# Three steps moved in the order of a one-core hybrid decoder layer: the first pair's scan products, the squares of the second hidden tile of a pair, and the first output transpose

## The chip, the cores and the metric

One core of a Trainium2 chip runs one inference step of a decoder layer. The metric is the device time of one execution in microseconds (us); lower is better. The kernel before takes 1161.29 us (median of three runs, 1161.14 to 1161.82).

## What is computed

512 prompt tokens and 8 sample tokens, 520 columns in all, go through one layer with a width of 1024. Cut to what matters here:

```python
proj = u @ w_in                      # u: normalized, modulated x
# branch B: xBC -> causal conv4 + SiLU -> x, B, C; chunked scan
states = einsum('bcsgn,bcsgr,bcsgrp->bcgrpn', B, decay_end, x)
y_diag = einsum('bcgrqs,bcsgrp->bcqgrp', wts, x)
y_off  = einsum('bcqgn,bcqgr,cbgrpn->bcqgrp', C, exp(acs), h_in)
x = x + gate1 * (merged @ w_o)
u2 = rmsnorm(x) * (1 + scale2) + shift2
x = x + gate2 * (square(relu(u2 @ w_mlp1)) @ w_mlp2)
out = rmsnorm(x)
```

The scan works on 32 heads in 16 pairs, in four chunks of 128 tokens. The hidden width of the MLP is 4096.

## The kernel before, in words

**Orientation.** Activations lie transposed: 128 features on the partitions, 520 tokens in the free dimension. Every float32 product is made of three products of a split into a high and a low part (`hi`, `lo` of the activations, `wh`, `wl` of the weights). ScalarE (ACT) copies the high part, VectorE (DVE) subtracts it for the low part.

**Windows and quarters.** The work is a list of windows (`win`, line 252), each the product of one 128-column weight block with all tokens. A window has four quarters of 12 matmuls (`one`, line 1306). After each quarter `run` (line 352) calls what was hung on it with `at` (line 349); a slot is 4 times the window's number plus the quarter. The dictionary `PLAN` (line 35) holds slots relative to a window. The engines' programs are in the order in which these calls are made: `manual_schedule` is set for all engines, and an engine that waits holds up all that is behind it on the same engine.

**The start of the scan.** Windows 4 and 5 make the x of pairs 0 and 1. Their evacuation `xbc_evac` (line 368) runs in the first quarter of the next window: two ACT copies out of PSUM and three DVE convolution steps. Then, by `PLAN`, come `finish` (a small DVE step on the samples' columns, then SiLU on ACT), `scan1`, `scan2` and `scan3`. `scan1` (line 435) transposes the pair's four chunks on TensorE into `ptx` and makes two DVE products, `xdec` (by `dd`, the decay to the chunk's end) and `xdt` (by dt). `scan2` (line 446) makes the chunk states `pst` from `xdec`, and `hc` from them (one ACT copy, six DVE steps). `scan3` (line 459) makes `pyd` and `pyo`, the latter from `hc`. `scan_w` (line 417) makes the decays between tokens: DVE subtracts, GpSimd (POOL) masks, ACT takes the exponential; `scan_m` (line 431) multiplies them by the masked products of B and C. For pair 0, `scan1` stands at 12 quarters behind window 4's start, in one slot with `scan_w(0)` and behind it.

**The MLP.** The first product of the MLP is made in four parts of 1024 hidden columns. In the last three of them (`f` = 1 to 3) two windows at a time are made by `seven` (line 1337) with seven half-size products, p = 0 to 6, four such pairs in each part. The products accumulate in three PSUM banks, y, x and w (`yb`, `xb`, `wb`), in the order y, x, w, y, x, w, x. Between them results are copied or added out: after p = 0 ACT copies y to `s1` (trace: `su`), after p = 1 and 2 DVE makes `u2_` and `s15`, after p = 3 ACT writes half of the first hidden tile `r0`, after p = 4, 5 and 6 DVE adds the rest of the hidden tiles `r1` and `r0`. As p = 3 goes on in bank y, it can't start before `s1` is copied. `squares` (line 1344) is three ACT instructions: ReLU, square, and the copy `hi`; `m1_lo` (line 790) is the DVE subtraction `lo`. A pair's weights are four blocks t = 0 to 3, split two products ahead by `split_s` (line 292); for t = 0 and t = 2, DVE first makes two sums of weight blocks (`ss`). The list `later` carries what is left over to the next pair or to `two` (line 1320), which makes the first two windows of the second product of the MLP.

The order of DVE around the end of a pair is: last addition to `r1`; `lo` of `r0`; two `wl` (t = 1); then, of the next pair, two `ss` (t = 2); `lo` of the last pair's `r1`; two `wl` (t = 2); `u2_`; `s15`; one `wl` (t = 3). The order of ACT is: squares of `r0`; two `wh` (t = 1); squares of `r1`; then, of the next pair, two `wh` from the sums (t = 2); the copy `su`; one `wh` (t = 3).

**The end.** `m2_evac` (line 803) adds the last part of the MLP to x in place (`x2`) and hangs up `finish_tile` (line 856): five transposes on TensorE and five small DVE products by the last norm's weight (`yo`). For output block 0 it stands in the last quarter of the second of the two windows of `two`, for blocks 1 and on in the second quarter of the window behind the block's own.

Of the kernel before, what the change touches and what calls it, by code (L numbers as in the profile page):

```python
# [34 lines left out]
PLAN = {'silu': [5, 10],  # L35
 'decay': [12, 15],
 'decay_load': 5,
 'mask': [14, 15],
 'tok': [12, 15],
 'state': [15, 21],  # L40
 'out': [19, 25],
 'bc_silu': [7, 7],
 'bc': [12, 12],
# [29 lines left out]
def tile_hybrid_step(  # L73
# [32 lines left out]
    def act(name, dtype=F32):  # L106
        return ap.tile([P, SLOT], dtype, name=nm(name), tag="act", bufs=NSLOT)
# [7 lines left out]
    def aux(name):  # L115
        return pp.tile([P, 512], F32, name=nm(name), tag="aux", bufs=4)
# [4 lines left out]
    def halves(ap_):  # L121
        return ap_.rearrange("p (h c) -> p h c", h=2)

    def chunks(ap_):
        return ap_.rearrange("p (c q) -> p c q", c=NC)

    def tt(out, in0, in1, op):
        V.tensor_tensor(out=out, in0=in0, in1=in1, op=op)  # L128

    def stt(out, in0, scalar, in1, op0=ALU.mult, op1=ALU.add):  # L130
        V.scalar_tensor_tensor(out=out, in0=in0, scalar=scalar, in1=in1, op0=op0, op1=op1)  # L131
# [7 lines left out]
    def a_copy(out, in_, func=AF.Copy, **kw):  # L139
        S.activation(out=out, in_=in_, func=func, **kw)  # L140

    def mm(out, lhsT, rhs, start=True, stop=True, **kw):
        PE.matmul(out, lhsT=lhsT, rhs=rhs, start=start, stop=stop, **kw)  # L143
# [105 lines left out]
    hooks, mid, end = {}, 1, 3  # L249
# [99 lines left out]
    def at(q, w, fn, *args):  # L349
        hooks.setdefault(4 * w + q, []).append((fn, args))  # L350
# [13 lines left out]
    xbc, szt = {}, {}  # L364
# [3 lines left out]
    def xbc_evac(ps, w, t):  # L368
        raw, cv = act("raw"), act("cv")
        views = ([(halves(raw[:, 0:T]), halves(cv[:, 0:T]), ps[:, :, 0:TH])] if not isinstance(ps, list) else  # L370
                 [(raw[:, h * TH:(h + 1) * TH], cv[:, h * TH:(h + 1) * TH], ps[h][:, 0:TH]) for h in range(2)])
        for r_, c_, p_ in views:
            a_copy(r_, p_)
            a_copy(c_, p_, AF.Identity, scale=par2[:, 72 + t:73 + t], bias=par("cbb", t))
        for k in (2, 1, 0):
            stt(cv[:, 3 - k:NP], raw[:, 0:NP - 3 + k], par2[:, 24 * k + t:24 * k + t + 1], cv[:, 3 - k:NP])
        V.tensor_copy(out=rst[:, :, t], in_=raw[:, NP - 3:T])
        xbc[t] = cv

        def finish():  # L380
            stt(cv[:, NP:T], raw[:, NP:T], par2[:, 72 + t:73 + t], pb[:, t, :])
            a_copy(cv[:, 0:T], cv[:, 0:T], AF.Silu)
            if t < 16:
                V.tensor_copy(out=xs_all[:, :, t], in_=cv[:, NP:T])
            else:
                g, dst = t % 4, bexp if t < 20 else cexp
                V.tensor_copy(out=dst[:, :, 4 * g:4 * g + 4], in_=cv[:, NP:T].unsqueeze(2).to_broadcast([P, NS, 4]))
        if t < 16:
            e = t % 2
            for key, f, args in (("silu", finish, ()), ("tok", scan1, (t,)), ("state", scan2, (t,)), ("out", scan3, (t,))):  # L390
                at(PLAN[key][e], w - e, f, *args)
        else:
            at(PLAN["bc_silu"][w > 4], w, finish)
            if t >= 20:
                at(PLAN["bc"][w > 4], w, bc_group, t - 20)
# [13 lines left out]
    scan, acb = {}, {}  # L409
# [5 lines left out]
            SY.dma_start(out=acb[j][h], in_=ascr[2 * j + h].partition_broadcast(P))  # L415

    def scan_w(j):
        st = scan[j] = {}
        pab = acb.pop(j)
        e2 = st["e2"] = act("e2")  # L420
        segs = st["seg"] = [act("seg") for _ in range(2)]
        for h in range(2):
            hd, rows, sv = 2 * j + h, slice(64 * h, 64 * h + 64), chunks(segs[h][:, 0:NP])
            tt(sv, chunks(pab[h]), acs[:, :, hd:hd + 1].to_broadcast([P, NC, P]), ALU.subtract)
            G.affine_select(out=sv, in_=sv, pattern=[[0, NC], [1, P]], compare_op=ALU.is_ge, fill=-1e30,  # L425
                            base=0, channel_multiplier=-1)
            a_copy(e2[rows, 0:384], pab[h][rows, P:NP], AF.Exp)
        for h in range(2):
            a_copy(segs[h][:, 0:NP], segs[h][:, 0:NP], AF.Exp)
# [3 lines left out]
            tt(seg[:, 0:NP], seg[:, 0:NP], cbm[j // 4][:, 0:NP], ALU.mult)  # L433

    def scan1(j):
        hv, xT_, st = slice(2 * j, 2 * j + 2), xbc[j], scan[j]
        ptx = aux("ptx")
        for c in range(NC):
            PE.transpose(ptx[:, c * P:(c + 1) * P], xT_[:, c * P:(c + 1) * P], ident)
        pv = ptx.rearrange("p (c h e) -> p c h e", c=NC, h=2)  # L440
        for key, f in (("xdec", dd), ("xdt", dtt)):
            st[key] = act(key)
            tt(st[key][:, 0:NP].rearrange("p (c h e) -> p c h e", c=NC, h=2), pv,
               f[:, 0:NC, hv].unsqueeze(3).to_broadcast([P, NC, 2, 64]), ALU.mult)
# [184 lines left out]
    def add_square(acc, t, first, n=T):  # L629
        d = acc if first else act("sqt")  # L630
        a_copy(d[:, 0:n], t[:, 0:n], AF.Square)
        if not first:
            tt(acc[:, 0:n], acc[:, 0:n], d[:, 0:n], ALU.add)
# [67 lines left out]
    def residual(x_, xo, ps, prm, o):  # L701
        t = small([P, NS], "rs")
        tt(t, ps[:, 1, NP - TH:TH], msm(prm, o), ALU.mult)
        tt(t, t, xo[:, NP:T], ALU.add)
        stt(halves(x_[:, 0:T]), ps[:, :, 0:TH], mp(prm, o), halves(xo[:, 0:T]))
        V.tensor_copy(out=x_[:, NP:T], in_=t)
# [83 lines left out]
    def m1_lo(r, hi, lo):  # L790
        tt(lo[:, 0:T], r[:, 0:T], hi.bitcast(F32)[:, 0:T], ALU.subtract)
        hm.append((hi, lo))
# [10 lines left out]
    def m2_evac(ps, w, o, half):  # L803
        residual(x2[o], x2[o], ps, 5, o)
        if half:
            if o == 0:
                sqf.insert(0, act("sqf"))
            add_square(sqf[0], x2[o], o == 0)
            if o == KT - 3:
                V.memset(vf, 1.0)  # L810
                at(end, w + 1, row_means, sqf, 1.0 / D, vf)
            at(mid if o else end, w + 1, finish_tile, o)

    sqf = []
    vf = const([P, 5], "vf")
# [100 lines left out]
    for f in range(4):  # L916
# [5 lines left out]
        for k in range(KT):  # L922
            win("m2", D * f, 256 * (k // 2), k % 2, lambda f=f: hm[8 * f:8 * f + 8],
                lambda ps, w, k=k, f=f: m2_evac(ps, w, k, f == 3))
# [156 lines left out]
    def par(key, i, n=1):  # L1081
        return par1[:, P1[key] + i:P1[key] + i + n]
# [217 lines left out]
    later = []  # L1300

    def evac(n):
        if wins[n][3]:
            wins[n][3](ps_of.pop(n), n)
# [32 lines left out]
    def seven(n):  # L1337
        y, x, w = (aux(z)[:, 0:TH] for z in ("yb", "xb", "wb"))
        banks = (y, x, w, y, x, w, x)
        su, s15, r0, r1 = act("su"), act("s15"), act("relu"), act("relu")  # L1340
        s1, u2_ = su[:, 0:TH], su[:, TH:T]
        hl = [(act("hi", F32R), act("lo", F32R)) for _ in range(2)]

        def squares(r, hi, c0):
            a_copy(r[:, c0:T], r[:, c0:T], AF.Relu)
            a_copy(r[:, 0:T], r[:, 0:T], AF.Square)
            a_copy(hi[:, 0:T], r[:, 0:T])

        def after(p):
            if p == 0:  # L1350
                a_copy(s1, y)
                while later:
                    later.pop(0)()
                evac(n - 1)
            elif p == 1:
                tt(u2_, x, s1, ALU.add)
            elif p == 2:
                tt(s15[:, 0:TH], w, s1, ALU.add)
            elif p == 3:
                a_copy(r0[:, 0:TH], y, AF.Relu)  # L1360
            elif p == 4:
                tt(r1[:, TH:T], x, s15[:, 0:TH], ALU.add)
            elif p == 5:
                tt(r0[:, TH:T], w, u2_, ALU.add)
                squares(r0, hl[0][0], TH)
            else:
                tt(r1[:, 0:TH], x, s1, ALU.add)
                m1_lo(r0, *hl[0])
                squares(r1, hl[1][0], 0)
                later.append(lambda: m1_lo(r1, *hl[1]))  # L1370

        for p in range(7):
            splits_to(unit_of[n] + p // 2 + 2, p % 2 == 1)
            (hi, lo), c = splits[n, p // 2], 4 * (p % 2)
            for k in range(4):
                xh, xl = terms[p][k]
                for i, (w_, x_) in enumerate(((hi, xh), (hi, xl), (lo, xh))):
                    mm(banks[p], w_[:, c + k, :], x_, p < 3 and k == 0 and i == 0, k == 3 and i == 2,
                       skip_group_check=True)
            after(p)  # L1380
            run(n + p // 4, p % 4)
        splits_to(unit_of[n] + 5)
        run(n + 1, 3)
# [61 lines left out]
```

## Time and profile before

| | |
|---|---|
| median of the runs | 1161.29 us |
| the profiled execution: time | 1163.04 us |
| the profiled execution: span from first to last instruction | 1161.3 us |
| TensorE busy (matmuls) | 1128.1 us, 97%, 9554 |
| VectorE busy | 809.0 us, 70%, 1566 |
| ScalarE busy | 497.5 us, 43%, 780 |
| GpSimd busy | 46.1 us, 4%, 85 |
| granted TensorE clock | 0.997 |

PE is TensorE, PEld its weight loads, DVE VectorE, ACT ScalarE, POOL GpSimd, SP SyncE. In a timeline a row gives the start (us), the duration (us), the engine, the line of the helper, the operation, what it writes and reads, and how many alike follow each other; in brackets how long the engine sat idle before it, and what ended that. As helpers record most operations, most rows have the same few lines, and the names of the tiles tell them apart. The profiled execution took 1.74 us more than its span.

### The profile page before, as it was taken

How to read it: one execution, taken by the hardware profiler on the slowest of the kernel's cores; microseconds unless marked ns; L12 is line 12 of the kernel's file. 1: busy time of each engine (PE TensorE's matmuls, PEld its weight loads, DVE VectorE, ACT ScalarE, POOL GpSimd, SP SyncE). 2: the span in 40 equal slices, each digit the busy share in tenths (PEclk: the TensorE clock that was granted, in tenths of full speed). 3: DMA queues.
4: the chain of work that ended last, by engine and by line, in shares of the span. 5: the costliest groups of instructions: out<-in, count | busy, mean ns of one | idle time of the engine just before them, and what ended most of it. 6: DMA issues, size and time to landing. Idle time of an engine off the chain costs nothing.

```text
span 1161.3 us, 22937 instructions
## 1 busy us (share of the span) xinstructions
PE 1128.1 (97%) x9554; PEld 1092.7 (94%) x9554; DVE 809.0 (70%) x1566; ACT 497.5 (43%) x780; POOL 46.1 (4%) x85
## 2 busy tenths in 40 slices
PE   6999999999999999999999999999999999999997
PEld 5798999999998888999999999999999999999996
DVE  5677888678888587888567334578777647657764
ACT  5456555455552222234443222345536515524622
POOL 3001111011110000000000000003000000000000
PEclk9999999999999999999999999999999999999999
DMA  9924333333348996567563243332222332332302
GB/s 280 326 74 132 114 115 96 94 112 114 114 147 292 324 329 199 178 187 212 171 230 101 95 165 124 114 124 97 81 96 73 109 110 73 109 110 73 104 7 74
DMA packets 137747, 164.96 MB, mean 142 GB/s; under 512 B 7144, under 2 KB 107961, under 8 KB 137636
## 3 DMA queue, kind: packets, MB, share of 16 engines
q1 hardware_dynamic: 137116, 162.85, 42.9%
q8 instruction: 75, 1.23, 0.4%
q0 software_dynamic: 528, 0.66, 0.2%
q14 instruction: 28, 0.23, 0.1%
HBM read 145.26 MB, written 18.45 MB: 141 GB/s over the span
## 4 chain that ended last, share of the span: by engine, by line
PE 83%; ACT 6%; DVE 6%; DMA 3%; issue 1%; SPq 1%; ACTq 0%; DVEq 0%
PE ps L143 72%; DMA wa<-in_w_ada_dram 2%; ACT wh L140 2%; DVE wl L128 2%; ACT relu L140 2%; PE xb L143 1%; PE pada L143 1%; PE pyd L143 1%; PE pst L143 1%; PE pyo L143 1%; PE yb L143 1%; ACT hi L140 1%; PE wb L143 1%; DVE cv L131 1%; DVE ss L128 1%
## 5 line engine op out<-in xcount | busy, mean ns | idle before, releaser
L143 PE MATMUL ps<-hi,wh 128*128 128x260 f32 (+2 forms) x2432 | 501.7, 286 | 2.4 <-ACT cv L140 1.1
L143 PE MATMUL ps<-lo,wh 128*128 128x260 f32 (+2 forms) x2432 | 493.3, 283 | 1.7 <-DVE lo L128 1.4
L143 PE MATMUL ps<-hi,wl 128*128 128x260 f32 (+2 forms) x2432 | 491.0, 282 | 0.0
L143 PEld LDWEIGHTS ps<-hi,wh 128*128 128x128 f32 x2432 | 375.2, 188 | 18.1 <-issue 13.6
L143 PEld LDWEIGHTS ps<-lo,wh 128*128 128x128 f32 x2432 | 376.5, 188 | 3.3 <-DVE lo L128 3.3
L143 PEld LDWEIGHTS ps<-hi,wl 128*128 128x128 f32 x2432 | 376.0, 188 | 0.0
L140 ACT ACTIVATE wh<-wt 128x1024 fp32r<-128x1024 f32 (+1 forms) x191 | 183.1, 960 | 318.3 <-PE ps L143 301.9
L128 DVE TENSOR_TENSOR wl<-wt,wh 128x1024 fp32r<-128x1024 f32 (+1 forms) x191 | 210.4, 1103 | 66.2 <-ACT wh L140 66.2
L131 DVE SCALAR_TENSOR_TENSOR cv<-raw,par,cv 128x511 f32<-128x511 f32 (+2 forms) x72 | 54.0, 750 | 10.9 <-ACT cv L140 9.0
L128 DVE TENSOR_TENSOR rs<-ps,mod 128x8 f32<-128x8 f32 x40 | 6.6, 164 | 62.4 <-PE ps L143 62.4
L140 ACT ACTIVATE wh<-ss 128x512 fp32r<-128x512 f32 x48 | 28.7, 621 | 31.7 <-PE ps L143 26.0
L143 PE MATMUL xb<-hi,wl 128*128 128x260 f32 x144 | 40.8, 283 | 0.0
L143 PE MATMUL xb<-hi,wh 128*128 128x260 f32 x144 | 40.7, 283 | 0.0
L143 PE MATMUL xb<-lo,wh 128*128 128x260 f32 x144 | 40.5, 282 | 0.0
L140 ACT ACTIVATE relu<-relu 128x520 f32<-128x520 f32 (+2 forms) x56 | 29.4, 525 | 20.0 <-DVE relu L128 19.2
L425 POOL TENSOR_SCALAR_AFFINE_SELECT seg<-seg 128x512 f32<-128x512 f32 x32 | 24.9, 801 | 299.6 <-DVE seg L128 243.9
L143 PE MATMUL yb<-hi,wh 128*128 128x260 f32 x96 | 28.1, 293 | 8.2 <-ACT su L140 8.2
L140 ACT ACT_TABLE_LOAD x27 | 34.6, 1283 | 2.9 <-DVE cv L131 1.7
L140 ACT ACTIVATE cv<-cv 128x520 f32<-128x520 f32 x24 | 15.3, 639 | 43.1 <-DVE cv L131 43.1
L128 DVE TENSOR_TENSOR wl<-ss,wh 128x512 fp32r<-128x512 f32 x48 | 31.8, 683 | 0.0
L143 PE MATMUL pada<-wa,cT 128*32 128x128 f32 (+1 forms) x384 | 29.0, 400 | 1.1 <-DMA wa<-in_w_ada_dram 0.9
L131 DVE SCALAR_TENSOR_TENSOR x<-ps,mod,x 128x520 f32<-128x520 f32 (+1 forms) x34 | 24.7, 727 | 5.7 <-PE ps L143 4.6
(312 smaller groups left out, 1332.9 us busy)
## 6 DMA issues: line engine op xcount, KB each, us to landing
wt<-in_w_in_dram SPq DMA_DIRECT2D x38, 1024.0 KB
wt<-in_w_mlp_dram SPq DMA_DIRECT2D x32, 1024.0 KB
wa<-in_w_ada_dram SPq DMA_DIRECT2D x96, 256.0 KB
acb<-ascr SPq DMA_DIRECT2D x32, 256.0 KB
hn<-in_state_ssm_dram SPq DMA_DIRECT2D x32, 256.0 KB
out_dram<-hn SPq DMA_DIRECT2D x32, 256.0 KB
wt<-in_w_b_out_dram SPq DMA_DIRECT2D x8, 1024.0 KB
gscr<-sg SPq DMA_DIRECT2D x16, 260.0 KB
```

The lines of the kernel that those rows point to most:

```text
L128: V.tensor_tensor(out=out, in0=in0, in1=in1, op=op)
L131: V.scalar_tensor_tensor(out=out, in0=in0, scalar=scalar, in1=in1, op0=op0, op1=op1)
L140: S.activation(out=out, in_=in_, func=func, **kw)
L143: PE.matmul(out, lhsT=lhsT, rhs=rhs, start=start, stop=stop, **kw)
L425: G.affine_select(out=sv, in_=sv, pattern=[[0, NC], [1, P]], compare_op=ALU.is_ge, fill=-1e30, base=0, channel_multiplier=-1)
```

## The change

Three things are moved. Nothing is added to or taken from the computation.

- `scan1` of pair 0 goes from 12 to 9 quarters behind window 4's start, from the slot behind `scan_w(0)` to one ahead of `finish` of pair 1.
- In `seven`, the squares of `r1` no longer stand at the end of their own pair but in the next one, behind the copy `su` (after p = 0); `lo` of `r1` goes from after p = 0 to after p = 2 of the next pair. Behind the last pair of a part both come after the first quarter of `two`.
- `finish_tile` of output block 0 goes to the slot of block 1's, ahead of it.

```diff
@@ PLAN
+ 'tok0': 9,
@@ xbc_evac
-                at(PLAN[key][e], w - e, f, *args)
+                at(PLAN["tok0"] if key == "tok" and t == 0 else PLAN[key][e], w - e, f, *args)
@@ scan_w
-        st = scan[j] = {}
+        st = scan.setdefault(j, {})
@@ scan1
-        hv, xT_, st = slice(2 * j, 2 * j + 2), xbc[j], scan[j]
+        hv, xT_, st = slice(2 * j, 2 * j + 2), xbc[j], scan.setdefault(j, {})
@@ m2_evac
-            at(mid if o else end, w + 1, finish_tile, o)
+            at(mid, w + (1 if o else 2), finish_tile, o)
@@ seven, after(p)
             if p == 0:
                 a_copy(s1, y)
-                while later:
+                if later:
                     later.pop(0)()
                 evac(n - 1)
             elif p == 1:
                 tt(u2_, x, s1, ALU.add)
             elif p == 2:
                 tt(s15[:, 0:TH], w, s1, ALU.add)
+                while later:
+                    later.pop(0)()
...
                 tt(r1[:, 0:TH], x, s1, ALU.add)
                 m1_lo(r0, *hl[0])
-                squares(r1, hl[1][0], 0)
+                later.append(lambda: squares(r1, hl[1][0], 0))
                 later.append(lambda: m1_lo(r1, *hl[1]))
```

## Rows read from the trace of the kernel before

**Rows 1.** The page, part 1: busy time and share of each engine.

```profile
PE 1128.1 (97%) x9554; PEld 1092.7 (94%) x9554; DVE 809.0 (70%) x1566; ACT 497.5 (43%) x780; POOL 46.1 (4%) x85
```

**Rows 2.** Waits: who waited for whom, us in total, times, longest.

```profile
PE yb L143 <- ACT su L140: 8.2, 9, 0.9
```

**Rows 3.** Timeline of PE, end of window 7 to the start of window 9.

```profile
100.16 1.16 PE L143 MATMUL pst<-xdec,btok 128*128 128x128 f32 x8 [2.22 <-DVE xdec L128]
...
108.47 0.94 PE L143 MATMUL pyo<-cv,hc 128*128 128x128 f32 x6
...
109.27 0.48 PE L143 MATMUL ps<-hi,wh 128*128 128x260 f32 x2
```

**Rows 4.** Timeline of DVE, the same stretch and what leads to it.

```profile
93.79 0.22 DVE L131 SCALAR_TENSOR_TENSOR cv<-raw,par,pb 128x8 f32<-128x8 f32 x1
...
99.43 0.68 DVE L128 TENSOR_TENSOR xdec<-ptx,dd 128x512 f32<-128x512 f32 x1
100.03 0.68 DVE L128 TENSOR_TENSOR xdt<-ptx,dtt 128x512 f32<-128x512 f32 x1
...
107.08 1.23 DVE L131 SCALAR_TENSOR_TENSOR hc<-hc,cd,pst 128x64 f32<-128x64 f32 x6
```

**Rows 5.** Timeline of ACT, the same stretch.

```profile
94.09 1.28 ACT L140 ACT_TABLE_LOAD   x1 [1.67 <-DVE cv L131]
...
106.32 0.26 ACT L140 ACTIVATE hc<-pst 128x128 f32<-128x128 f32 x1
...
107.89 0.60 ACT L140 ACTIVATE sz<-ps 128x520 f32<-128x520 f32 x1
```

**Rows 6.** Windows: length, then busy us (count) of PE, PEld, DVE, ACT, POOL.

```profile
872.60:882.67 10.07, 10.07 (x86) 10.07 (x85) 7.18 (x15) 4.36 (x9) 0.00 (x0) 1.00 0.31 100
...
1079.07:1090.30 11.23, 10.31 (x84) 10.11 (x85) 9.80 (x20) 7.92 (x16) 0.00 (x0) 1.00 0.28 95
```

**Rows 7.** Timeline of PE, p = 3 of the last pair of the third part.

```profile
1090.30 0.39 PE L143 MATMUL yb<-hi,wh 128*128 128x260 f32 x1 [0.92 <-ACT su L140]
```

**Rows 8.** Timeline of ACT, from the end of one pair into the next.

```profile
1084.26 1.09 ACT L140 ACTIVATE relu<-relu 128x260 f32<-128x260 f32 x2 [1.25 <-DVE relu L128]
...
1086.97 1.29 ACT L140 ACTIVATE relu<-relu 128x520 f32<-128x520 f32 x2
1088.30 0.64 ACT L140 ACTIVATE hi<-relu 128x520 fp32r<-128x520 f32 x1
1088.84 1.13 ACT L140 ACTIVATE wh<-ss 128x512 fp32r<-128x512 f32 x2
1089.88 0.36 ACT L140 ACTIVATE su<-yb 128x260 f32<-128x260 f32 x1
1090.15 0.62 ACT L140 ACTIVATE wh<-wt 128x512 fp32r<-128x512 f32 x1
```

**Rows 9.** Timeline of DVE, the same stretch.

```profile
1083.80 0.42 DVE L128 TENSOR_TENSOR relu<-wb,su 128x260 f32<-128x260 f32 x1
...
1086.05 0.70 DVE L128 TENSOR_TENSOR lo<-relu,hi 128x520 fp32r<-128x520 f32 x1 [0.51 <-ACT hi L140]
1086.67 0.68 DVE L128 TENSOR_TENSOR wl<-ss,wh 128x512 fp32r<-128x512 f32 x1
...
1088.48 0.68 DVE L128 TENSOR_TENSOR ss<-wt,ss 128x512 f32<-128x512 f32 x1
1089.08 0.69 DVE L128 TENSOR_TENSOR lo<-relu,hi 128x520 fp32r<-128x520 f32 x1
...
1091.57 0.68 DVE L128 TENSOR_TENSOR wl<-wt,wh 128x512 fp32r<-128x512 f32 x1
```

**Rows 10.** Timeline of PE, transposes of output block 1.

```profile
1112.84 0.66 PE L864 MATMUL pt<-ident,x 128*128 128x128 f32 x4 [1.48 <-DVE x L131]
```

**Rows 11.** Timeline of DVE, output blocks 0 and 1.

```profile
1110.65 0.88 DVE L128 TENSOR_TENSOR yo<-pt,gbc 128x128 f32<-128x128 f32 x4
...
1112.02 0.76 DVE L131 SCALAR_TENSOR_TENSOR x<-ps,mod,x 128x520 f32<-128x520 f32 x1
```

## The prediction

> **What bounds the kernel now.** I read the page's busy times first: TensorE is busy 97% of the span, so time is to be had only where it stands idle [rows 1]. The view of waits names where it waits for another engine: nine times for ScalarE's copy `su`, in all 8.2 us, each about 0.9 [rows 2]. There are twelve pairs in `seven`, four in each of three parts; nine of them have another pair ahead, so it is one wait for each boundary between pairs, at p = 3, as the last of them at 1090.30 shows [rows 7]. The timeline of PE shows two more long waits that the diff touches: 2.22 us for `xdec` ahead of the first `pst` [rows 3], and 1.48 us for the updated x ahead of the transposes of output block 1 [rows 10]. These three places are all that the change can win from, some 13 us with the restarts. What matters is what comes last behind each wait once the named one is gone, so for each I laid the queues of DVE and ACT out in the new order, with the durations and steps of the rows; an engine works its instructions off in the order written.
>
> **The boundary between pairs (the large term).** The change takes three ACT instructions, the squares of `r1`, from ahead of `su` and puts them behind it. The windows view says who is full there: from one stall to the next, 11.23 us, DVE is busy 9.80 and ACT 7.92; a first pair, which has no stall, takes 10.07 [rows 6]. So I follow DVE. Call the start of its second `ss` S (1088.48). Its end, S + 0.68, releases the second of the two `wh` copies that stand ahead of `su` on ACT. Before, this copy starts one step behind the first (1.13 for both, less 0.62 for one: 0.51), at 1089.35, or S + 0.87, because the squares had kept ACT until 1088.84 [rows 8, 9]. Without them it starts when the sum is there, with 0.03 for the hand-over (1083.80 + 0.42 to 1084.26 is one) at S + 0.71, and `su` at S + 1.23 where it was S + 1.40. **The stall shrinks by 0.17 us only**: `su` is late because of the sums, and these because of DVE's queue.
>
> Now what the move delays. Behind `su` come the squares: the first starts 0.27 after `su` (1089.88 to 1090.15), the copy `hi` 1.33 behind it (1086.97 to 1088.30) and lasts 0.64 [rows 8]: `hi` ends at S + 3.47. On DVE `lo` of `r1` now stands behind `s15` and needs that `hi`, so it starts at S + 3.51, and the next `wl` 0.62 later (1086.05 to 1086.67), at S + 4.13. Before, this `wl` started at 1091.57, S + 3.09 [rows 9]. So **everything behind it on DVE comes 1.04 us later**: two `ss`, the addition to `r1`, two `wl`, the last addition to `r0`. Is there slack to take it up? From that addition on (1083.80) the row of releases is closed: ACT's squares of `r0` wait for it (1.25 idle, until 1084.26), DVE's `lo` of `r0` waits for their `hi` (0.51 idle, until 1086.05), then two `wl`, two `ss` follow without a pause to S, and S releases `su` again [rows 8, 9]. The other idle time of DVE in the period, for the last product in bank x, lies beside the squares of `r0` and is not in this row. So the period from `su` to `su` grows from 11.23 to about 12.27, and TensorE follows it: at the first boundary of a part it is 0.17 early, at the second 0.87 late, at the third 1.91 late. Part of it will show as a new wait: the addition to `r1` out of bank x, 1.04 later on DVE, must end before p = 6 may write there. In a part's fourth pair no `ss` are made for what follows, and the loop ends. Three parts: 3 x 1.91 = **+5.7 us**. At `two`, the squares come one `wh` later, and their `hi` and `lo` are wanted only by the last quarters of its two windows, six quarters on: nothing, as long as that cover holds; without it what the same move costs at a boundary, about 1 us for each part.
>
> The rows name ACT as the releaser of this stall. The Trainium skill, Perfetto Trace Analysis, Optimization Strategy, says to find the semaphore on which the gap's engine waits and to make that dependency start sooner. By it alone, taking work from ahead of `su` would give back all nine stalls; by the row of releases 0.17 each. I go by the second, since the releaser of `su`'s own predecessor is a row of DVE; the first is a rival below.
>
> **The start of the scan.** Four transposes and two DVE products move three quarters up; no DMA moves with them, and SP and POOL are passed by none. On TensorE the transposes cost nothing, wherever they stand, as long as TensorE waits for another engine behind them, which it will by 2 us or more; without that cover half a microsecond (four like them last 0.66 [rows 10]). `pst` then finds `xdec` ready, and its 2.22 us of waiting go [rows 3]. But on DVE the two products, a step of 0.60 each (99.43 to 100.03), now stand ahead of `finish` of pair 1 (93.79) [rows 4]. Behind that step ACT waits idle: its table load for the SiLU came 1.67 us late because of it [rows 5]. So ACT's queue from 94.09 on starts 1.20 later. ACT has no pause worth naming before the next weight copy, and behind that the subtractions of `scan_w(1)`, the mask on POOL, the exponentials, the copy `hc` and DVE's six `hc` steps hang on one another; the two products were in a gap of DVE there, waiting for ACT, so their going wins nothing. The copy `hc` moves from 106.32 to 107.52, the six steps from 107.08 to 108.28, ending at 109.51 [rows 4, 5]. TensorE reaches `pyo` 8.3 us behind the start of `pst` (100.16 to 108.47), at about 105.7 now, and waits there for `hc` until 109.5, and the next window for its PSUM bank, which ACT's `sz` frees 1.20 later than before, at 109.69. It starts at about 109.74 where it was 109.27 [rows 3, 5]: **+0.5 us**. The bounds: -2.4 if nothing on ACT were late, +1.2 if TensorE took over the whole delay. I take the value of the two releases named.
>
> **The output transposes.** They move behind a window's first half on TensorE, and their five DVE products with them. Before, block 1's transposes waited until x was updated (1112.02 + 0.76, start 1112.84), and that update stood behind the five products on DVE [rows 10, 11]. These take 0.20 each (0.88 for four, of which the last is 0.28 long), so the update comes 1.0 earlier. TensorE gets there no later than before: the half microsecond of block 0's transposes leaves ahead of the window and comes back ahead of block 1's. What is late next is the same update, half a microsecond of waiting. The ten products then follow in a row on DVE, under the window's other half, and would have to be a window late to be felt. **-1.0 us**, between 0 and -1.5 (all of the wait).
>
> **The sum.** +5.7 + 0.5 - 1.0 = +5.2. On the profiled execution's own time, 1163.04 with a span of 1161.3, that is 1168.2; this execution took 1.75 us more than the median of 1161.29. Against the median: **1166.4 us**, 0.44% more. About 0.2%, 2.3 us, is what a measurement of this kernel can tell from no change.
>
> **Rivals.** *The stalls go* (the rule named above). If `su` were held by the squares alone, nine stalls of 11.23 - 10.07 = 1.16 us would go [rows 6], and with the outputs' -1.0 and at best -2.4 in the scan the time is 1147 to 1151. For it: the wait's name, and ACT's squares right ahead of the two `wh`. Against: the second `ss` ends at 1089.16, 0.7 before `su` starts, so 0.17 is all there is. It decides if DVE's sums were ready before the squares end. Chance 0.07. *The loop takes it up.* If some other slack in the period, as DVE's 11.23 - 9.80 = 1.43 us idle [rows 6], is in the row of releases after all, the boundary costs nothing or a little: 1160 to 1163. Against: both its pauses are accounted for. Chance 0.09. *Only the scan is wrong*: `finish` of pair 1 isn't what ACT waits for, -2.4 for +0.5, 1163.5; chance 0.05. *The delay reaches further*, into the fourth pair or the quarters of `two`: 1 us more for each part, 1169.5; chance 0.04. That the change doesn't do what it says has no place: the order written is the order run. The forecast has 0.75.
>
> **The numbers.** Slower by over 0.2% are the forecast, the farther delay, half of the scan's rival, and a part of the loop's: 0.83. Within 0.2%: 0.09. Faster: 0.08. (The loop's rival lies within 0.2% but for 0.02, the scan's is halved between slower and the same.) The forecast alone, with 0.5 us for each part and the scan's upper bound, lies at 1164.9 to 1168.2. The range takes in the scan's rival and the upper end of the loop's, and leaves out the first rival, most of the loop's and the farther delay: 1162.8 to 1168.2.
>
> **What would show it.** Right: nine waits of `yb` for `su` remain, the first of each part near 0.75, the others near 1.4; the period is near 12.3; DVE waits some 0.8 for `hi` ahead of `lo` of `r1`, once in each boundary; six new waits of `xb` for a DVE addition; no wait at `pst` but one of about 2 at `pyo` for `hc`; `pt` still waits, about 0.5. Wrong: the waits for `su` are gone, or the period falls below 11.23, or `pyo` runs without a wait.

## The result and the profile after

The changed kernel is slower. In the first comparison its median is 1169.12 us (1168.70 to 1169.26, four executions) beside 1161.55 us for the kernel before (1161.14 to 1162.33, four): a ratio of 1.0064, 95% interval 1.0046 to 1.0081. A second one (below) gives 1.0054, 1.0041 to 1.0066. The forecast was slower, by 5.2 us to 1166.4; the sign and the mechanism held, the time lies outside the range of 1162.8 to 1168.2. The two profiled executions differ by 5.66 us, 1163.04 and 1168.70, with spans of 1161.3 and 1166.9. One execution of the last kernel below took 2814.06 us and is left out of its ratio.

The page of the changed kernel, part 1 (it answers to [rows 1]; lines from 40 on are one higher, by the new entry of PLAN):

```profile
PE 1129.9 (97%) x9554; PEld 1093.6 (94%) x9554; DVE 810.2 (69%) x1566; ACT 497.4 (43%) x780; POOL 45.9 (4%) x85
```

The instructions are the same in number. TensorE's idle time, span less busy time, grows from 33.2 to 37.0 us, and its busy time by 1.8. The six periods with the new wait below have about 0.3 us more of busy time each for the same matmuls (the window below: 10.61, and 10.31 in [rows 6]).

Its view of waits (to [rows 2]):

```profile
DVE lo L129 <- ACT hi L141: 51.0, 60, 4.7
...
PE yb L144 <- ACT su L141: 9.9, 9, 1.3
...
PE xb L144 <- DVE relu L129: 2.4, 6, 0.4
```

The nine waits of `yb` for `su` that the change was aimed at are all there and have grown, 8.2 to 9.9 us; six new ones of `xb` for an addition on DVE have come.

**The boundary between pairs.** Windows of the changed kernel, nearly one period of the third part, columns as in [rows 6]:

```profile
1084.72:1096.99 12.27, 10.61 (x84) 10.23 (x84) 9.96 (x19) 7.93 (x17) 0.00 (x0) 1.00 0.26 87
```

From `yb` to `yb` the period is 12.29 us (1084.78 to 1097.07 below) where it was 11.23, as DVE does the same work with longer pauses in it. The timeline of PE (to [rows 7]): the first `yb` of the third part, then the second, the `xb` behind it, and the third.

```profile
1072.49 0.39 PE L144 MATMUL yb<-hi,wh 128*128 128x260 f32 x1 [0.74 <-ACT su L141]
...
1084.78 0.39 PE L144 MATMUL yb<-hi,wh 128*128 128x260 f32 x1 [1.29 <-ACT su L141]
...
1089.74 0.36 PE L144 MATMUL xb<-hi,wh 128*128 128x260 f32 x1 [0.39 <-DVE relu L129]
...
1097.07 0.39 PE L144 MATMUL yb<-hi,wh 128*128 128x260 f32 x1 [1.29 <-ACT su L141]
```

The first wait of the part is shorter than the 0.92 of [rows 7], the others longer. Now the two queues around the second of them. Timeline of ACT (to [rows 8]):

```profile
1083.28 1.17 ACT L141 ACTIVATE wh<-ss 128x512 fp32r<-128x512 f32 x2 [1.59 <-DVE ss L129]
1084.36 0.37 ACT L141 ACTIVATE su<-yb 128x260 f32<-128x260 f32 x1
1084.62 1.30 ACT L141 ACTIVATE relu<-relu 128x520 f32<-128x520 f32 x2
1085.96 0.64 ACT L141 ACTIVATE hi<-relu 128x520 fp32r<-128x520 f32 x1
...
1091.17 1.09 ACT L141 ACTIVATE relu<-relu 128x260 f32<-128x260 f32 x2 [1.25 <-DVE relu L129]
```

and of DVE (to [rows 9]):

```profile
1083.10 0.69 DVE L129 TENSOR_TENSOR ss<-wt,ss 128x512 f32<-128x512 f32 x1
...
1086.63 0.70 DVE L129 TENSOR_TENSOR lo<-relu,hi 128x520 fp32r<-128x520 f32 x1 [0.72 <-ACT hi L141]
1087.24 0.68 DVE L129 TENSOR_TENSOR wl<-wt,wh 128x512 fp32r<-128x512 f32 x1
...
1090.71 0.42 DVE L129 TENSOR_TENSOR relu<-wb,su 128x260 f32<-128x260 f32 x1
```

S, the start of the second `ss`, is 1083.10. ACT had stood idle for 1.59 us when the sums released `wh`: the squares are gone from ahead of `su`, and ACT waits in their place. `su` starts at S + 1.26, where it was S + 1.40; the prediction said S + 1.23. Then `lo` of `r1` waits 0.72 for `hi` and starts at S + 3.53 (said: 3.51), the next `wl` at S + 4.14 (4.13, before 3.09). From there ACT's 1.25 of idle time ahead of the squares of `r0` is what it was in [rows 8]: the delay passes through whole.

**The scan's start.** Timeline of PE (to [rows 3]):

```profile
97.11 1.05 PE L144 MATMUL pst<-xdec,btok 128*128 128x128 f32 x8
...
107.56 0.49 PE L144 MATMUL pyo<-cv,hc 128*128 128x128 f32 x2 [1.77 <-ACT hc L141]
108.52 0.87 PE L144 MATMUL pyo<-cv,hc 128*128 128x128 f32 x4 [0.47 <-DVE hc L132]
...
109.47 0.51 PE L144 MATMUL ps<-hi,wh 128*128 128x260 f32 x2
```

The 2.22 us at `pst` are gone; 1.77 + 0.47 = 2.24 us stand at `pyo` instead, and the next window starts 0.20 later than in [rows 3], though this execution had come to the stretch 0.26 us earlier (a row of PE ahead of all that was moved starts at 86.20, where it was 86.46). So the scan's part costs 0.46 us here, where +0.5 was forecast. Timeline of DVE and of ACT (to [rows 4, 5]):

```profile
93.54 0.68 DVE L129 TENSOR_TENSOR xdec<-ptx,dd 128x512 f32<-128x512 f32 x1
94.14 0.68 DVE L129 TENSOR_TENSOR xdt<-ptx,dtt 128x512 f32<-128x512 f32 x1
94.74 0.21 DVE L132 SCALAR_TENSOR_TENSOR cv<-raw,par,pb 128x8 f32<-128x8 f32 x1
```

```profile
95.03 1.28 ACT L141 ACT_TABLE_LOAD   x1 [2.86 <-DVE cv L132]
...
107.25 0.26 ACT L141 ACTIVATE hc<-pst 128x128 f32<-128x128 f32 x1
```

The two products stand ahead of `finish`, ACT's idle time ahead of the table load grows from 1.67 to 2.86, by 1.19 (said: 1.20), and the copy `hc` comes 12.22 behind the table load, as it came 12.23 behind it before.

**The outputs.** Timeline of PE (to [rows 10, 11]): 1.48 us of waiting have become 0.39.

```profile
1118.57 0.66 PE L865 MATMUL pt<-ident,x 128*128 128x128 f32 x4 [0.39 <-DVE x L132]
```

### The profile page after: what moved, and what is told of

Its sections match the earlier page's. It is cut to its first block, busy times and chain, and to the rows that moved or that the text cites. A ratio compares the mean times of both kernels' runs of the same rounds, so it can differ in the third digit from the quotient of the medians.

```text
span 1166.9 us, 22927 instructions
## 1 busy us (share of the span) xinstructions
PE 1129.9 (97%) x9554; PEld 1093.6 (94%) x9554; DVE 810.2 (69%) x1566; ACT 497.4 (43%) x780; POOL 45.9 (4%) x85
## 3 DMA queue, kind: packets, MB, share of 16 engines
q8 instruction: 75, 1.23, 0.4%
## 4 chain that ended last, share of the span: by engine, by line
PE 82%; DVE 7%; ACT 5%; DMA 3%; issue 1%; SPq 1%; POOL 0%; ACTq 0%; POOLq 0%; DVEq 0%
PE ps L144 71%; DVE wl L129 3%; DMA wa<-in_w_ada_dram 2%; PE xb L144 1%; ACT relu L141 1%; PE pada L144 1%; PE pyd L144 1%; PE yb L144 1%; PE pyo L144 1%; ACT wh L141 1%; PE pst L144 1%; DVE ss L129 1%; DVE lo L129 1%; ACT hi L141 1%; SPq L216 1%
## 5 line engine op out<-in xcount | busy, mean ns | idle before, releaser
L129 DVE TENSOR_TENSOR lo<-relu,hi 128x520 fp32r<-128x520 f32 x32 | 22.4, 700 | 20.9 <-ACT hi L141 20.6
L144 PEld LDWEIGHTS xb<-hi,wh 128*128 128x128 f32 x144 | 27.1, 189 | 3.4 <-issue 3.4
```

## The experiments

Two questions. Is it DVE's sums that hold `su`, and would the squares' move pay without them? And where do the medians get more than the 5.66 us between the profiles? Differences in us below are the ratio's excess times 1162.7, about the median of the kernel before in these comparisons.

**The same kernel again.** No edit.

> The kernel before once more, unchanged. The two profiled executions so far differ by 5.66 us, the medians of the same comparison by 7.6. Theory (the profiled execution of before was a long one): a second profiled execution of the same kernel comes out nearer to its median of 1161.3 to 1161.6, at 1161 to 1162 where it was 1163.04, with the difference in the first 60 us, ahead of everything the change touches; the ratio of the medians is 1.000 within 0.001. Rival (the change costs some 2 us that its profiled execution does not show): the profile is again at about 1163, 1.5 above the median, stretch by stretch as before.

Ratio 0.9999 (0.999 to 1.0008). The second profile took 1163.55 us, longer than the first: the expectation of 1161 to 1162 fell, 1163.04 was no outlier. What was out of line are the medians at the head of this document. Over the three comparisons the kernel before was run 66 times: 1160.78 to 1165.59, median 1162.66. Single executions are thus spread over 4 us, and medians of three and four of 1161.29 and 1161.55 are low draws.

**The changed kernel again.** No edit.

> The changed kernel once more, unchanged, for its time against before with more executions. Theory (the rows give +5.7, and on top the granted clock falls to half for some 3.3 us behind the new wait at pyo in nearly every execution, as in the scan's kernel alone, where before it falls behind the pst wait in about half of them): +6 to +7.5 us, and the mean clock of most executions is 0.996 or 0.997 where before has 0.998 in half. Rival (the first comparison drew fast executions of before, and there is nothing beside the rows): +5.0 to +5.7, clocks as before.

Ratio 1.0054 (1.0041 to 1.0066), +6.3 us (4.8 to 7.7), 1168.80 us. The interval holds the 5.66 of the profiles and the forecast's 5.2. Three of its five executions have a mean clock of 0.998, so the part about the clock fell; of all nine, four have 0.998, beside 27 of 66 of the kernel before with 0.998 or more. That the change draws more clock falls is not shown: the kernels below with the scan alone and with the outputs alone have one of eleven each, and no run says why. All nine executions of the changed kernel have a median of 1168.99, 6.3 above the 1162.66.

**One part at a time.** The boundary alone, that is, in `seven`:

```
         if p == 0:
-            while later:
+            if later:
...
         elif p == 2:
+            while later:
+                later.pop(0)()
...
-            squares(r1, hl[1][0], 0)
+            later.append(lambda: squares(r1, hl[1][0], 0))
```

> The boundary between pairs alone: squares of r1 behind su, lo of r1 behind s15. Theory (the row of releases through DVE): +5.7 us by the prediction's working, +6.0 by the trace of the changed kernel, so 1167 to 1168; the nine waits for su remain, the first of each part near 0.75, the others near 1.3; six waits of xb for DVE's addition. Rival (the squares are what holds su, the loss of the whole came from the scan or the outputs): 1151, no waits for su. Rival (half of the loss is elsewhere): +3.

Ratio 1.0056 (1.0043 to 1.0068), +6.5 us (5.0 to 7.9). The nine waits are there, 9.9 us in all, 0.76 and 1.28 in the third part, and the six of `xb`. The boundary carries the loss; both rivals fall.

The scan's start alone (`'tok0': 9` and what it needs):

> The scan's start alone: the four transposes and the two DVE products of tile 0 three quarters sooner. Theory: the 2.2 us of waiting at pst go and come back at pyo as about 2 us for hc, +0.5 us by the working, +0.65 by the trace of the changed kernel: 1161.8 to 1162.3. Rival (finish of pair 1 is not what ACT waits for): -2.4, 1159. Rival (the part of the loss that the profiles do not show is here): +2.5, 1164.

Ratio 1.0011 (1.0002 to 1.002), +1.3 us (0.2 to 2.3): a small loss, no gain. The wait is at `pyo`, 1.79 us for `hc` and 0.47 behind it. The -2.4 rival falls, and the one of +2.5 lies just outside the interval. The granted clock fell behind the wait in this profile (0.50 from 108 to 110 us), so part of the 1.3 can be the clock's.

The outputs alone (`at(mid, w + (1 if o else 2), finish_tile, o)`):

> The output transposes of block 0 alone, behind the first half of the second window. Theory: -1.0 us, 1160.4; the wait of pt for the updated x falls from 1.5 to about 0.5 us and stays with the same releaser. Rival (the ten products in a row on DVE hold the next window): 0 or above. Rival (all of the wait goes): -1.5.

Ratio 0.9997 (0.9988 to 1.0006): the time cannot tell -1.0 from nothing. The wait can, in the timeline of PE of this kernel:

```profile
1111.49 0.66 PE L864 MATMUL pt<-ident,x 128*128 128x128 f32 x4 [0.40 <-DVE x L131]
```

1.48 before, 0.40 now, as forecast. The three parts add up to 6.5 + 1.3 - 0.3 = 7.5, within the intervals of the whole.

**The scan a quarter later,** so that the products stand behind `finish` on DVE (`'tok0': 10`):

> The scan's start alone, with the four transposes and two products a quarter later than in the change, so that on DVE they stand behind finish of pair 1. Theory (in the change they held finish, with it ACT's SiLU and in the end hc): the wait at pst goes or is under 0.5, the wait at pyo stays small, -0.3 to -0.5 us against before in the trace's steps. Rival (what comes late at pyo is TensorE's own new order, not DVE's): +0.5 as with the change. The clock: where TensorE has no stall of 2 us at 98 to 112 us, no fall of the granted clock is to be seen there (it fell to half for some 3.3 us behind the pst wait in one execution of the boundary's kernel, and behind the pyo wait in the scan's).

Ratio 1.0001 (0.9992 to 1.001). The wait at `pst` is gone and the table load is back at its 1.67 us of idle time, so it was the two products that held `finish`, as the prediction said. TensorE still waits 1.33 + 0.47 at `pyo`, and the expected gain of 0.3 to 0.5 did not come: nothing brings `hc` forward, and most of the wait moves from one place to the other. The part on the clock fell: in this execution it was half behind that wait (108 to 110 us: 0.50).

**The sums out of DVE's queue.** In `split_s`, of the kernel before and then of the changed kernel:

```
         def total(i, x, y, op):
             sums[i] = act("ss")[:, 0:512]...
-            tt(sums[i], x, y, op)
+            G.tensor_tensor(out=sums[i], in0=x, in1=y, op=op)
```

> The kernel before, with the sums of every pair (the four ss of a pair, s and the like) added on GpSimd, out of DVE's queue; nothing else. It takes some 0.4 to 0.7 us off DVE for each sum, 2 us or more in each period. Theory (two rows of releases of nearly one length: su is held by the sums through DVE, and right behind these, 0.17 us, by ACT's squares ahead of wh): about the time of before, -0.1 to -1.5 us; the nine waits for su stay near 0.9, with ACT's squares now alone in front. Rival (DVE's occupancy alone is the bound of the period, so relief of DVE is enough): nine waits go, -9 to -10 us, 1152.

> The changed kernel, with the same sums on GpSimd. Theory (the move of the squares is right, but only once the sums no longer wait in DVE's queue): the nine waits for su go, and the whole is 9 to 11 us below before, 1151 to 1153, that is 15 to 17 below the changed kernel; lo of r1 still waits for hi but nobody waits for it. Rival (it is the squares' later end, lo of r1 and the addition in bank x that set the period of the changed kernel, sums or no sums): waits of xb and yb stay, 1162 or above. Rival (GpSimd's additions are so long that they hold wh in DVE's place): above 1165.

With the squares at their old place: ratio 1.0038 (1.0025 to 1.005), +4.4 us, where -0.1 to -1.5 was expected. With the squares moved: 0.9973 (0.9961 to 0.9984), -3.1 us, 1160.08 against 1162.70. The view of waits of the first still has the nine,

```profile
PE yb L143 <- ACT su L140: 8.1, 9, 1.2
```

and its timeline of ACT at such a boundary says why:

```profile
1081.76 1.29 ACT L140 ACTIVATE relu<-relu 128x520 f32<-128x520 f32 x2
1083.09 0.64 ACT L140 ACTIVATE hi<-relu 128x520 fp32r<-128x520 f32 x1
1083.63 1.13 ACT L140 ACTIVATE wh<-ss 128x512 fp32r<-128x512 f32 x2
1084.67 0.36 ACT L140 ACTIVATE su<-yb 128x260 f32<-128x260 f32 x1
```

None of these rows has idle time ahead of it, here and at the other eight boundaries: with the sums out of the way it is ACT's own squares that hold `su`. The expectation was right on the waits; what it left out, the price of sums on GpSimd, is shown below. In the second kernel no wait of PE for `su` is left in the view of waits, and its windows show TensorE busy without a break across the last two boundaries of the third part:

```profile
1075.00:1098.00 23.00, 23.00 (x194) 23.00 (x193) 16.86 (x29) 18.82 (x34) 0.00 (x0) 1.00 0.32 108
```

So there are four cases: neither moved, the waits stand; squares moved, they stand and grow; sums moved, they stand; both moved, all nine are gone. Two rows of releases of nearly one length ended at `su`, and the change shortened one. The Trainium skill, Perfetto Trace Analysis, Optimization Strategy, has the reader find the semaphore behind a gap and make that dependency start sooner; by the name of the wait alone that would have been the nine waits, some 10 us. The trace agrees only where the question is asked again of the instructions ahead of `su`, on both engines.

The gain was expected at 9 to 11 us and is 3. The reason is seen when the timelines of POOL and of DVE of this kernel are laid side by side, here behind the first boundary of the first part:

```profile
891.24 1.67 POOL L299 TENSOR_TENSOR ss<-wt 128x512 f32<-128x512 f32 x1 [1.24 <-DVE wl L129]
892.87 1.77 POOL L299 TENSOR_TENSOR ss<-wt,ss 128x512 f32<-128x512 f32 x1
```

```profile
891.68 0.41 DVE L129 TENSOR_TENSOR su<-xb,su 128x260 f32<-128x260 f32 x1
892.02 0.41 DVE L129 TENSOR_TENSOR s<-wb,su 128x260 f32<-128x260 f32 x1
892.36 1.10 DVE L129 TENSOR_TENSOR lo<-relu,hi 128x520 fp32r<-128x520 f32 x1
893.38 1.79 DVE L129 TENSOR_TENSOR wl<-wt,wh 128x512 fp32r<-128x512 f32 x1
895.10 0.42 DVE L129 TENSOR_TENSOR relu<-xb,s 128x260 f32<-128x260 f32 x1
```

While GpSimd adds, DVE's `wl` takes 1.79 us instead of the 0.68 of [rows 9], and `lo` 1.10 instead of 0.70; the additions out of a PSUM bank keep their 0.41. The Trainium skill, GPSIMD Engine Reference, Specifications, says that GpSimd shares its SBUF interfaces with VectorE, with contention for DVE instructions that have two SBUF inputs. The rows agree: `wl` and `lo` have two such inputs, `su<-xb,su` has one. Not every `wl` beside a sum is slowed:

```profile
871.44 1.83 POOL L299 TENSOR_TENSOR ss<-wt,ss 128x512 f32<-128x512 f32 x1
```

```profile
871.42 0.68 DVE L129 TENSOR_TENSOR wl<-ss,wh 128x512 fp32r<-128x512 f32 x1
872.02 1.79 DVE L129 TENSOR_TENSOR wl<-wt,wh 128x512 fp32r<-128x512 f32 x1
```

The first `wl` keeps its 0.68, and the sum beside it takes 1.83, where the shortest sums of this kernel take 1.29; the second takes 1.79. The rows look as if the two engines took turns.

The sums of a part's first pair run ahead of it, beside DVE's work for the windows that come there, and TensorE pays. In the first part two `lo` there take 1.79 and 1.80 us (0.69 each in the kernel before), the update of x behind them comes late, and a window waits for it, where the kernel before has no wait:

```profile
858.90 1.79 DVE L129 TENSOR_TENSOR lo<-tc,hi 128x520 fp32r<-128x520 f32 x1
860.61 1.80 DVE L129 TENSOR_TENSOR lo<-td,hi 128x520 fp32r<-128x520 f32 x1
```

```profile
863.63 0.47 PE L144 MATMUL ps<-hi,wh 128*128 128x260 f32 x2 [1.67 <-DVE x L132]
888.91 0.39 PE L144 MATMUL wb<-hi,wl 128*128 128x260 f32 x1 [0.33 <-DVE wl L129]
895.66 0.36 PE L144 MATMUL xb<-hi,wh 128*128 128x260 f32 x1 [0.38 <-DVE relu L129]
```

The last two waits come back in each of the three parts. The kernel with the squares at their old place has the wait for x too, 1.68 us at 864.51.

**Squares behind, `lo` at the end.** An edit of the kernel before: the squares of `r1` go behind `su` and one `wh` on ACT, and `lo` of `r1` behind the addition of p = 4 on DVE:

```
             if p == 0:
...
-                while later:
-                    later.pop(0)()
...
             elif p == 2:
...
+                if later:
+                    later.pop(0)()
...
                 tt(r1[:, TH:T], x, s15[:, 0:TH], ALU.add)
+                while later:
+                    later.pop(0)()
...
-                squares(r1, hl[1][0], 0)
+                later.append(lambda: squares(r1, hl[1][0], 0))
```

> The boundary alone in another order: the squares of r1 on ACT as late as in the change or later (behind the copy of y for p = 2's wh), and lo of r1 on DVE put behind the addition after p = 4, so that DVE does not wait for hi. Theory (DVE's queue with the sums is the row of releases, and the squares' place in ACT's decides only how long DVE stands in it): the loss shrinks but does not turn into a gain: +1 to +3 us against before; nine waits for su of 0.7 to 1.5 remain. Rival (the whole loss is DVE's wait for hi, and without it the squares' move pays): -5 to -10.

Ratio 1.0017 (1.0008 to 1.0026), +2.0 us. DVE waits for `hi` there no more; the nine waits remain, and the loop is shorter than the change's:

```profile
1079.04:1090.78 11.74, 10.46 (x86) 10.21 (x85) 9.99 (x19) 7.91 (x15) 0.00 (x0) 1.00 0.30 91
```

11.74, about halfway between 11.23 and 12.29. So half of what the change adds to the period goes where DVE need not wait for `hi` ahead of `lo` of `r1`; without that wait the squares' move still does not pay. The sums have stayed in DVE's queue.

**The better kernel.** The changed kernel with sums on GpSimd and `'tok0': 12`, the scan's start as it was:

> The boundary and the output transposes as in the change, the sums on GpSimd, and the scan's start as before. Theory (the scan's part is a loss of its own): 0.6 to 1.7 us below the changed kernel with sums on GpSimd, so 1158 to 1159.5, some 4 below before; the stall of 2 us ahead of the first pairs (at 862 us) and those of 0.6 at the first boundaries stay. Rival (the scan's part costs nothing): equal to it, 1160.

Ratio 0.9969 (0.9958 to 0.998), 1158.96 us, 3.6 below the kernel before and faster than both. It isn't told apart from the one with the earlier scan (0.9973): their intervals overlap.

**The clock.** In the timeline of PE of the boundary's kernel, at the scan's start, whose code is that of the kernel before:

```profile
99.35 2.04 PE L143 MATMUL pst<-xdec,btok 128*128 128x128 f32 x8 [2.23 <-DVE xdec L128]
101.18 1.06 PE L439 MATMUL ptx<-ident,cv 128*128 128x128 f32 x4
```

The same eight products took 1.16 us in [rows 3], behind a wait of 2.22. The windows of this execution show what differed: PEclk, the last column but two, is below 1.00, where the profile of the kernel before has 1.00 throughout these 6 us:

```profile
98.00:100.00 2.00, 0.65 (x3) 0.65 (x4) 2.00 (x5) 1.78 (x4) 1.61 (x2) 0.86 0.03 13
100.00:102.00 2.00, 2.00 (x12) 2.00 (x11) 1.76 (x3) 1.98 (x4) 0.00 (x0) 0.50 0.00 0
102.00:104.00 2.00, 2.00 (x16) 2.00 (x15) 1.85 (x3) 0.35 (x1) 0.63 (x1) 0.79 0.07 15
```

The granted clock fell to half, 1.2 GHz, and came back; TensorE lost about 0.28 + 1.00 + 0.42 = 1.7 us (each window's length times what is missing from 1). The timelines agree: this execution was 0.82 us ahead of the profile of the kernel before at 74 us, and 0.82 behind it at 112 us, with the same code in between. Two kernels try to take the cause away, by seven products of `ident` with itself inside the wait, of the changed kernel ahead of `pyo` (into that bank) and of the kernel before ahead of `pst`, as shown (their result is overwritten):

```
+        for _ in range(7 if j == 0 else 0):
+            mm(pst[:, 0:P], ident, ident)
```

> The changed kernel with seven products of ident with itself ahead of the first pyo of pair 0, some 1.7 us of work inside TensorE's wait of 2.0 for hc; their result is overwritten. Theory (the stall makes the clock fall): no fall at 106 to 113 us, 0.5 to 1.5 us below the changed kernel, and the mean clock up by 0.001. Rival (the fall does not come from the stall, or the fill holds pyo up): the same or slower.

> The kernel before with seven such products ahead of the first pst of pair 0, inside TensorE's wait of 2.2 for xdec. Theory: the falls at 98 to 104 us, that about half of the executions have, go; 0.3 to 1.0 us below before, and fewer executions with a clock of 0.997. Rival (the falls come elsewhere): no difference in time or clocks.

1.0045 (1.0031 to 1.0058) beside 1.0054 of the changed kernel, and 0.9997 (0.9988 to 1.0006): neither can be told from the kernel without the filling, though neither profile shows a fall in the stretch. What the falls cost on average is thus below what these runs can tell, and whether filling the wait keeps the clock up stays open: the two profiles of the changed kernel and the two of the kernel before show no fall there either.

## Why the prediction was wrong

- **The sum laid on the median: the step that failed.** The prediction had two bases and showed both: on the profiled execution's own time the sum made 1168.2, on the median of 1161.29 it made 1166.4, and it took the second. The 1161.29 stood on three executions; 66 have a median of 1162.66, 1.4 higher. On that the same +5.2 gives 1167.9, inside the range, and a range moved up by as much would have held 1169.12. The range was made of mechanisms alone: the spread of executions, over 4 us, had no place in it. Its upper end is not added up rightly either: 1166.4, 0.5 for each part and 0.7 for the scan's upper bound make 1168.6, not 1168.2. Of the 2.7 us between 1166.4 and 1169.12 the base is half.
- **The boundary, +5.7: right in every step, mis-sized by some 0.6.** S + 1.26, 3.53 and 4.14 for 1.23, 3.51 and 4.13; the period 12.29 for 12.27; first waits of 0.74, others of 1.29; 0.72 of DVE for `hi`; six waits of `xb`. The first boundary of the first part lies 0.29 us later than before (888.04 and 888.33), the last of the third 6.77 (1090.30 and 1097.07); the first wait is 0.16 shorter, so the boundaries cost 6.77 - 0.29 - 0.16 = 6.3 in these two profiles. Two periods of 12.29 and the 0.16 give 1.96 for each part, 5.9 for three; the last 0.4 come in between the parts, in small steps with no wait, and were not followed. The kernel with this part alone has 6.1 in its profile, by the same reckoning, and took 6.5 (5.0 to 7.9).
- **The scan, +0.5: the mechanism right, the size within the error.** `finish` 1.19 late, `hc` with it, the wait moved to `pyo`: 0.46 at the next window. By 887 us another 0.25 has come in small steps without a wait. The kernel with the scan alone has such steps too: against the kernel before it is 0.10 us late at 112 us and 0.34 at 687; why stays open. Measured alone, +1.3 (0.2 to 2.3).
- **The outputs, -1.0: right.** The wait fell by 1.09 us, to 0.39 for "half a microsecond". The time of this part alone doesn't show it.
- **The rivals.** *The stalls go* needed the sums ready before the squares ended; the kernel with sums on GpSimd and squares moved is that case, and there they do go. *The loop takes it up* falls with the period of 12.29. *Only the scan is wrong* falls with the scan's own run. *The delay reaches further*, 1 us more for each part, was nearest to the measured time, but not its cause: the rows have at most some 0.2 for each part between its last boundary and the next part's first.

The sum in the rows, 6.3 + 0.7 - 1.0 = 6.0, beside 5.2 forecast and 6.3 between the medians of nine and 66 executions. Between the two profiled executions it is 5.66, as that of the changed kernel came to the scan 0.26 earlier, ahead of all that was changed. Some 0.8 of the error is in the terms, the boundary's above all; 1.4 is in the base, and what is left is within the spread of single executions.

## What to carry to other kernels

A wait names the last instruction of a chain; before moving what stands ahead of it, ask when every other input of that chain would have been there, on each engine, because two chains of nearly one length need both to be cut. An instruction moved behind another delays its own readers: follow them until they come round to the place where you began, since in a loop of releases a delay of one microsecond is paid in every period. And when a sum is laid on a median of a few executions, put their spread into the range.

## What was not expected of the hardware

GpSimd's additions out of SBUF can slow DVE's beside them: 1.79 us for 0.68 with two SBUF inputs, and no change, 0.41, for an addition with one input in PSUM. Taking 0.68 us off DVE for a sum can so cost it 1.1 on the instruction next to it. GpSimd's own sums took 1.67 and 1.77 us there, 1.83 where a `wl` beside it kept its 0.68, and 1.29 at the least.

The granted clock is not the same from one execution to the next at the same place of the same code: behind the wait of 2.22 or 2.23 us at `pst` it fell to 1.2 GHz in three of the seven profiles that have this wait and stayed at 2.4 GHz in four; one fall cost about 1.7 us. At `pyo` it fell behind a wait of 1.33 + 0.47, and behind one of 1.76 to 1.79 + 0.47 in two of four profiles. Of the 66 executions of the kernel before, 27 have a mean clock of 0.998 or more and a median of 1161.70 us, the other 39 one of 1163.21. That the falls make this difference of 1.5 us is likely by its size, but no run here shows it.
